# Fixing TensorE's written order through a block's heads, with split products in place of transposes

## The chip, the core and the metric

The kernel runs on one core of a Trainium2 chip. The metric is the time of one execution in microseconds (us) on the device, as a median of runs. PE is TensorE, PEld its weight loads, DVE is VectorE, ACT is ScalarE, POOL is GpSimd and SP is SyncE, which issues the DMAs of the weights.

## What is computed

Two transformer-like blocks on a sequence of 256 tokens with 2048 features, all in float32. The change lies in block 1's mixing stage, whose reference is, cut down:

```
h = rms_norm(x, ln1)
qkv_a, beta_a, decay_a, z_a, qkv_b, gate_a, gate_b = split(h @ w_in)
y_a = gated_deltanet(qkv_a, beta_a, decay_a, z_a, ...) @ w_branch_a
y_b = attention(rope(q_b), rope(k_b), v_b) @ w_branch_b
x = x + (sigmoid(gate_a) * y_a + sigmoid(gate_b) * y_b) @ w_out
```

`gated_deltanet` has 8 heads of 128 features. q, k and v come out of a causal convolution of width 4 and a SiLU; q and k are normed. Each head has per-token factors: beta (a sigmoid) and a decay g, whose running sum within a chunk is gc. Per chunk a triangular matrix built from k k^T, beta and exp(gc_i - gc_j) is inverted, and the state runs over the chunks. The head's output is normed and multiplied by silu(z). Attention has 8 heads too, causal, with one block of keys. A feed-forward part follows, and then the second block.

## The kernel before, in words

**Products.** Every large product is made from split operands: a weight chunk (512 KB, `load_w`, L322 to L326) is loaded on SP's queue into one of three buffers, ACT copies it rounded to `hi` (L325) and DVE subtracts to get `lo` (L326). The activations are held split as well. `wide_steps` makes 256 output columns feature-major: for each of 16 tiles of the contraction and each of two halves one product of 512 columns with `hi` and one of 256 with `lo` (L379, L381). `group_steps` makes 512 output columns token-major with three products of 512 columns each (L351 to L353). Both are generators. A yield tells how much PE work has been issued, 1.0 for a 512-column and a 256-column product together, and 2.0 for three of 512. Their results lie in one of two two-bank buffers (`pp`); small products use four single banks (`ps`).

**Fill.** The heads are long chains of small operations over PE, ACT and DVE. Between the steps of a chain the program issues large products of other tensors: `Fill` (L399 on) holds a list `todo` of such generators, `pull(n)` runs the first ones until `n` units of work are issued, `between(steps)` runs a chain and pulls as many units as each step yields, and `upto(gen)` finishes a generator.

**Order.** The program gives an order and a priority by it. The order on each engine is chosen by the compiler's scheduler, which simulates the engines and takes the first instruction in program order that is ready.

**Block 1's heads.** `gdn_proj(half)` makes q, k and v for four heads (two 256-column parts each for q, k and v) with a convolution per 128 features (`conv_silu`, L469 to L473: one ACT operation, three of DVE at L472, a SiLU). `z_proj(half)` makes silu(z) for four heads with 63 units. `gdn_gates` makes a 16-column product, transposes it (L524), computes beta and g on DVE and ACT (L526 to L552) and sums g by two products (L554, L555). `gdn_half(half)` then runs:

- `gdn_scales`: squares on ACT (L567), sums by products of one column (L571), and `rsqrt` on a 128x16 tile (L574 to L582), a chain of 13 short DVE operations to the factor `bk` (L579);
- four times `gdn_pre`: per head six transposes of a broadcast column (L592, L594), which spread gc, bk and rq over the rows of a PSUM tile; a masked exponential and three DVE operations that end in `aq` (L597 to L607);
- `inverse16`: the four heads' matrices go to DRAM and come back with one 16x16 block per partition; 15 steps of DVE (L707, L709) invert them; they return through DRAM into `Z`, and POOL spreads `Z` into `X` (L726);
- `gdn_inverse` in rounds over two head pairs: products and DVE steps that build the 64- and 128-row inverses (L735 to L770);
- `gdn_post` for two head pairs: seven steps (L628 to L670). After L651 comes the norm: squares on ACT, `rsqrt` on DVE, the scaling by silu(z) (L663), and then the transposes (L667).

The sequence (L903 on) is: `gdn_proj(0)`, gates, the other parameters, rope's angles; then z0, g1 (`gdn_proj(1)`) and z1 as fill for half 0; a0 and a1 (`attn_proj`) as fill for half 1 and heads 0 to 3 of attention; and `branch_a` (a gate product and a product that reads `oah` and `oal`, the heads' outputs) as fill for heads 4 to 7.

Of the kernel before, what the change touches and what calls it, by code (L numbers as in the profile page):

```python
# [122 lines left out]
def two_blocks_kernel(ctx: ExitStack, tc: tile.TileContext, I: dict, out: bass.AP):  # L123
# [29 lines left out]
    def c(name, lo=0, hi=128):  # L153
        return tabs[name][lo:hi]

    load_consts(0, cpool, nc.sync)
    ident, one = c("ident"), c("one")

# [17 lines left out]
    def tm(tag, F, dt=F32, bufs=2, p=128, pool=None):  # L176

        shape = list(F) if isinstance(F, (tuple, list)) else [F]
        n = math.prod(shape)
        line = {"tiny": LINE // 2, "rcol": LINE // 2, "PC": LINE // 4}.get(tag, LINE)  # L180
# [67 lines left out]
    def tiny(shape):  # L248
        return tm("tiny", shape, bufs=8)

# [148 lines left out]
    class Fill:  # L399
# [18 lines left out]

        def upto(self, gen):
# [11 lines left out]
    fills = Fill()  # L431

# [45 lines left out]
    def gdn_proj(half):  # L478
        kq[half] = [Q(3 * half + j, shape=(128, 2, 2, 2, 128), name="gdkq") for j in range(2)]
        vv[half] = Q(3 * half + 2, name="gdv")  # L480
        for j, part in enumerate("qkv"):
# [7 lines left out]
            def take(m, p):  # L489
# [6 lines left out]
            yield from wide_steps(w_in, f0 * 128, 512, xs, factors, take, place_x if r1 is None else None)  # L496
# [18 lines left out]
    def gdn_gates():  # L515
        ab = tm("cva", T, bufs=3)[:16]
        wide(w_in, 3072, 16, xs, None, lambda m, p: act(ab, p, AF.Copy))
        hp = wk("hp", (2, 8), bufs=1)
# [32 lines left out]
        for i in range(2):  # L551
            stt(g[:, i], t0[:, i], -1.0, ea, ALU.mult, ALU.mult)  # L552
        p = psum()
# [6 lines left out]
        stt(nbe, beta, -1.0, eg, ALU.mult, ALU.mult)  # L560

    def gdn_scales(half):
# [16 lines left out]
        tt(out=bk, in0=beta[:, :, hs], in1=rk, op=ALU.mult)  # L579
        tt(out=kdr, in0=kds[:, :, hs], in1=rk, op=ALU.mult)  # L580
        tt(out=nber, in0=nbe[:, :, hs], in1=rk, op=ALU.mult)
        tt(out=egq, in0=eg[:, :, hs], in1=rq, op=ALU.mult)  # L582
        return rk, rq, bk, kdr, nber, egq

    def gdn_pre(h, scales):
        half, m = divmod(h, 4)
        rk, rq, bk, kdr, nber, egq = scales
# [12 lines left out]
        tt(out=mg, in0=ga.unsqueeze(2).to_broadcast([128, 2, 2, 128]), in1=pb, op=ALU.mult)  # L600
# [19 lines left out]
    def gdn_post(h, scales, pre):  # L620
        half, m = divmod(h, 4)
        rk, rq, bk, kdr, nber, egq = scales
# [41 lines left out]
        yield  # L664
# [8 lines left out]
    def gdn_half(half):  # L673
        sc = gdn_scales(half)
        yield 12
# [165 lines left out]
    for _ in gdn_proj(0):  # L841
        pass
    load_consts(1, quad, nc.sync)
    gdn_gates()
# [63 lines left out]
    fills.add(a0, a1)  # L908
    fills.between(gdn_half(1))
    fills.upto(a0)  # L910
    fills.between(rounds(attn_head(h) for h in (0, 1)))
    fills.between(rounds(attn_head(h) for h in (2, 3)))
    fills.upto(a1)
    ba = [branch_a(j) for j in range(4)]
    fills.add(*ba)
    fills.between(rounds(attn_head(h) for h in (4, 5)))
    fills.between(rounds(attn_head(h) for h in (6, 7)))
    fills.upto(ba[3])
# [534 lines left out]
```

## Time and profile before

| | us |
|---|---|
| median of 3 runs | 2841.1 |
| lowest and highest of them | 2834.95, 2859.62 |
| the profiled execution | 2833.93 |
| its span, first to last instruction | 2832.2 |

The profile is of one execution. Its page gives the busy time of each engine and cuts the span into 40 equal slices. Groups of instructions are named by line and by the program's tile names, `out<-in`. A busy PE is modelled, since its products are pipelined: a 512-column product is shown with some 0.39 us, though the next starts 0.23 us after it. Start times, or the pieces on the chain of waits, show the rate. PEclk is the granted share of 2.4 GHz.

### The profile page before, as it was taken

What the parts mean: (1) busy time and instruction counts of PE and PEld (TensorE: products, weight loads), DVE (VectorE), ACT (ScalarE), POOL (GpSimd) and SP (SyncE); (2) the same over time, 40 slices, a digit from 0 to 9 for tenths busy, and PEclk for the clock granted to TensorE, in tenths of its full rate; (3) what the DMA queues carried; (4) which work ended last, traced back from release to release, by engine and by line L of the source; (5) the groups of instructions that cost most, each with busy time, mean ns of one, the idle gap of its engine ahead of it and who ended that gap; (6) DMA issues with size and microseconds to landing.
All of it is one profiled execution on the core that took longest, in us unless ns stands there. A gap on an engine that the chain in (4) does not pass through costs nothing.

```text
span 2832.2 us, 40520 instructions
## 1 busy us (share of the span) xinstructions
PE 2767.0 (98%) x15538; PEld 2329.3 (82%) x15538; DVE 1856.2 (66%) x2908; ACT 1397.8 (49%) x2088; POOL 159.2 (6%) x217
## 2 busy tenths in 40 slices
PE   9999989999999999999999999899999999999997
PEld 7888877888888888888887777777888888888886
DVE  7786766555577755775666696876765655656565
ACT  6664545444455544554455544334543444434454
POOL 0003200000000000000001120230000000000001
PEclk9999999999999999999999999899999999999999
DMA  7565644666566656655656363253566666666554
GB/s 218 165 177 150 173 137 119 185 187 186 186 186 189 191 189 188 187 187 190 203 188 183 101 159 108 77 142 105 176 192 193 187 191 191 188 193 204 186 186 149
DMA packets 398200, 487.94 MB, mean 172 GB/s; under 512 B 38426, under 2 KB 283173, under 8 KB 398005
## 3 DMA queue, kind: packets, MB, share of 16 engines
q1 hardware_dynamic: 397221, 482.93, 56.5%
q8 instruction: 122, 2.00, 0.3%
q10 hardware_dynamic: 608, 2.11, 0.2%
q0 software_dynamic: 176, 0.30, 0.1%
q14 instruction: 73, 0.60, 0.1%
HBM read 479.25 MB, written 6.03 MB: 171 GB/s over the span
## 4 chain that ended last, share of the span: by engine, by line
PE 91%; DVE 4%; DMA 2%; ACT 1%; issue 1%; POOL 1%; SPq 0%; DVEq 0%; POOLq 0%; ACTq 0%
PE pp L379 28%; PE pp L381 15%; PE pp L351 14%; PE pp L352 14%; PE pp L353 14%; DVE lo L326 1%; PE ps L267 1%; DMA Z<-s 0%; PE ps L742 0%; DMA raw<-in_w_down_dram 0%; PE ps L1215 0%; PE ps L735 0%; DVE L L1149 0%; PE ps L1217 0%; POOL X L726 0%
## 5 line engine op out<-in xcount | busy, mean ns | idle before, releaser
L326 DVE TENSOR_TENSOR lo<-raw,hi 128x1024 fp32r<-128x1024 f32 x902 | 1108.7, 1229 | 808.0 <-ACT hi L325 784.1
L325 ACT ACTIVATE hi<-raw 128x1024 fp32r<-128x1024 f32 x902 | 953.6, 1057 | 1195.1 <-PE pp L352 554.1
L379 PE MATMUL pp<-xhl,hi 128*128 128x512 f32 x3648 | 1291.7, 397 | 2.1 <-DVE z L388 2.1
L381 PE MATMUL pp<-xhl,lo 128*128 128x256 f32 x3648 | 1030.9, 283 | 2.3 <-DVE lo L326 2.3
L379 PEld LDWEIGHTS pp<-xhl,hi 128*128 128x128 f32 x3648 | 684.0, 188 | 164.7 <-DVE z L388 2.4
L381 PEld LDWEIGHTS pp<-xhl,lo 128*128 128x128 f32 x3648 | 688.8, 189 | 10.2 <-issue 4.7
L353 PE MATMUL pp<-lo,hid 128*128 128x512 f32 x864 | 338.2, 391 | 0.5 <-DVE lo L326 0.5
L351 PE MATMUL pp<-hi,hid 128*128 128x512 f32 x864 | 338.3, 392 | 0.0
L352 PE MATMUL pp<-hi,hid 128*128 128x512 f32 x864 | 337.6, 391 | 0.0
L353 PE MATMUL pp<-lo,xhl 128*128 128x512 f32 (+1 forms) x544 | 206.4, 379 | 0.0
L352 PE MATMUL pp<-hi,xhl 128*128 128x512 f32 (+1 forms) x544 | 206.3, 379 | 0.0
L351 PE MATMUL pp<-hi,xhl 128*128 128x512 f32 (+1 forms) x544 | 206.2, 379 | 0.0
L353 PEld LDWEIGHTS pp<-lo,hid 128*128 128x128 f32 x864 | 162.3, 188 | 35.9 <-DVE lo L326 1.0
L351 PEld LDWEIGHTS pp<-hi,hid 128*128 128x128 f32 x864 | 162.3, 188 | 35.1 <-ACT hi L325 0.3
L352 PEld LDWEIGHTS pp<-hi,hid 128*128 128x128 f32 x864 | 162.4, 188 | 34.3
L351 PEld LDWEIGHTS pp<-hi,xhl 128*128 128x128 f32 x544 | 102.6, 189 | 18.7
L352 PEld LDWEIGHTS pp<-hi,xhl 128*128 128x128 f32 x544 | 102.6, 189 | 18.4
L353 PEld LDWEIGHTS pp<-lo,xhl 128*128 128x128 f32 x544 | 102.5, 188 | 18.3
L933 DVE TENSOR_TENSOR x<-x,pp 128x512 f32<-128x512 f32 x96 | 61.6, 683 | 31.7 <-PE pp L353 31.7
L388 DVE TENSOR_TENSOR z<-pp,z 128x512 f32<-128x512 f32 (+2 forms) x119 | 80.8, 679 | 1.3 <-ACT z L387 1.1
L390 DVE TENSOR_TENSOR z<-z,rstd 128x512 f32<-128x512 f32 x114 | 78.4, 688 | 3.3
L287 POOL TENSOR_TENSOR junk<-x,rows 128x512 f32<-128x512 f32 x8 | 13.4, 1670 | 1110.2 <-ACT junk L284 1110.2
(415 smaller groups left out, 2535.7 us busy)
## 6 DMA issues: line engine op xcount, KB each, us to landing
raw<-in_w_in_dram SPq DMA_DIRECT2D x244, 512.0 KB, 3.6
raw<-in_w_up_dram SPq DMA_DIRECT2D x176, 512.0 KB, 4.4
raw<-in_w_ffn_up_dram SPq DMA_DIRECT2D x128, 512.0 KB, 3.7
raw<-in_w_ffn_down_dram SPq DMA_DIRECT2D x128, 512.0 KB, 4.1
raw<-in_w_down_dram SPq DMA_DIRECT2D x88, 512.0 KB, 3.7
raw<-in_w_out_dram SPq DMA_DIRECT2D x64, 512.0 KB, 3.7
raw<-in_w_ple_gate_dram SPq DMA_DIRECT2D x32, 512.0 KB, 3.9
raw<-in_w_branch_a_dram SPq DMA_DIRECT2D x16, 512.0 KB, 3.7
```

Of the source, the lines that this page charges most:

```text
L267: nc.tensor.transpose(p[:w, m - m0, i * 128:(i + 1) * 128], src[:, i, 128 * m:128 * m + w], ident)
L287: nc.gpsimd.tensor_tensor(out=y, in0=s, in1=self.w2[j], op=ALU.mult)
L325: act(h, r, AF.Copy)
L326: tt(out=l, in0=r, in1=h.bitcast(F32), op=ALU.subtract)
L351: mm(p, xh, h[:, j], start=(k == 0), stop=False, skip_group_check=True)
L352: mm(p, xl, h[:, j], start=False, stop=False, skip_group_check=True)
L353: mm(p, xh, l[:, j], start=False, stop=last, skip_group_check=True)
L379: mm(P[:w, m].rearrange("p a b -> p (a b)"), h[:, j, f], x2.rearrange("p a b -> p (a b)"), start=(k == 0), stop=False, skip_group_check=True)
L381: mm(P[:w, m, 0], l[:, j, f], x2[:, 0], start=False, stop=last, skip_group_check=True)
L388: tt(out=z, in0=P[:w, :nw, 0], in1=z, op=ALU.add)
L390: tt(out=z, in0=z, in1=r()[:w].unsqueeze(1).to_broadcast([w, nw, T]), op=ALU.mult)
L933: tt(out=s, in0=s, in1=p, op=ALU.add)
```

## The change

- `pe_in_order()` opens a stretch, from the gates to the last `branch_a`, in which PE's instructions keep the order in which the program issues them. The other engines' order is still the scheduler's.
- The numbers that steps yield are new, and some steps yield that did not: the gates 6, 40 and 0; the scales 4 for each of four squares, 14 and 4; after `inverse16` 88 in place of 55; and 6 per head more at the norm of `gdn_post`.
- `gdn_gates` moves behind the other parameters and rope's angles, and runs with fill between its steps.
- The fill of half 0 is g1's six parts, now six generators, then z0 and z1. When `inverse16` has been issued, `fills.first(z0, z1)` puts z0 and z1 right behind the part that is under way.
- The token factors are no longer spread by transposes of broadcast columns. POOL gathers gc, bk and rq of four heads in a table `S`; two transposes turn it, ACT and DVE split it into `RT` (hi and lo), and per head and factor two products of 256 columns, with a broadcast column of a rounded identity (`picks`) as the weights, spread a row of it. The six transposes per head go.
- Two small tiles (`nacc`, `oka`) are padded less, and the squares of `gdn_scales` have two buffers (tag A) in place of one (tag E).

```diff
+    picks = cpool.tile([128, LINE], F32R, tag="picks", name="picks")
+    nc.scalar.activation(picks, ident[:, :LINE], AF.Copy)
...
+    def spread_table(S):
+        p = psum()
+        for i in range(2):
+            nc.tensor.transpose(p[:, i * 128:(i + 1) * 128], S[:, i], ident)
+        RT = wk("RT", (2, T), F32R, bufs=1)
+        split(RT[:, 0], RT[:, 1], p[:, :T])
+        return RT
+
+    def spread_row(p, RT, sel):
+        mm(p, sel, RT[:, 0], start=True, stop=False, skip_group_check=True)
+        mm(p, sel, RT[:, 1], start=False, stop=True, skip_group_check=True)
...
+        def first(self, *gens):
+            self.todo = self.todo[:1] + list(gens) + [g for g in self.todo[1:] if g not in gens]
...
+    def pe_in_order():
+        return tc.manual_schedule(engines={mybir.EngineType.PE})
...
-            yield from wide_steps(w_in, f0 * 128, 512, xs, factors, take, place_x if r1 is None else None)
+            for o in range(2):
+                yield wide_steps(w_in, f0 * 128 + 256 * o, 256, xs, factors, lambda m, p, o=o, take=take: take(2 * o + m, p),
+                                 (lambda k, o0, o=o: place_x(k, o)) if r1 is None else None)
...
     def gdn_gates():
         ab = tm("cva", T, bufs=3)[:16]
         wide(w_in, 3072, 16, xs, None, lambda m, p: act(ab, p, AF.Copy))
+        yield 6
...
+        yield 40
         p = psum()
         mm(p[:, 0:16], c("upper"), g, start=True, stop=True)
...
     def gdn_scales(half):
...
-            sq = wk("E", (2, 2, 128), bufs=1)
+            sq = wk("A", (2, 2, 128))
             act(sq, kq[half][m // 2][:, m % 2], AF.Square)
+            yield 4
...
+        S = wk("E", (2, 128), bufs=1)
+        nc.gpsimd.memset(S, 0.0)
+        nc.gpsimd.tensor_copy(S[:, :, 0:4], gc[:, :, hs])
+        nc.gpsimd.tensor_copy(S[:, :, 4:8], bk)
+        nc.gpsimd.tensor_copy(S[:, :, 8:12], rq)
...
-        return rk, rq, bk, kdr, nber, egq
+        yield 14
+        RT = spread_table(S)
+        yield 4
+        return (rk, rq, bk, kdr, nber, egq), RT
...
     def gdn_pre(h, scales):
...
-        pa, pb = psum((2, 128)), psum((2, 2, 128))
-        for i in range(2):
-            nc.tensor.transpose(pa[:, i], gc[:, i, h:h + 1].to_broadcast([128, 128]), ident)
-            for j, f in enumerate((bk, rq)):
-                nc.tensor.transpose(pb[:, i, j], f[:, i, m:m + 1].to_broadcast([128, 128]), ident)
+        pa, pb = psum(T), psum((2, T))
+        for j, p in enumerate((pa, pb[:, 0], pb[:, 1])):
+            spread_row(p, RT, picks[:, 4 * j + m:4 * j + m + 1].to_broadcast([128, 128]))
...
     def gdn_post(h, scales, pre):
...
             stt(ot[:, i], ot[:, i], ro[:, i:i + 1], zs[half][:, i, 128 * m:128 * m + 128], ALU.mult, ALU.mult)
-        yield
+        yield 6
...
-    def gdn_half(half):
-        sc = gdn_scales(half)
-        yield 12
+    def gdn_half(half, *light):
+        sc = yield from gdn_scales(half)
         pre = []
         for m in range(4):
             pre.append(gdn_pre(4 * half + m, sc))
             yield 5
         Z = inverse16([p[0][:, 0] for p in pre], 2)
-        yield 55
+        fills.first(*light)
+        yield 88
         for _ in rounds(gdn_inverse(pre[m:m + 2], Z[:, m:m + 2]) for m in (0, 2)):
             yield 6
         for m in (0, 2):
-            for _ in rounds(gdn_post(4 * half + m + i, sc, pre[m + i]) for i in range(2)):
-                yield 5
+            for n in rounds(gdn_post(4 * half + m + i, sc, pre[m + i]) for i in range(2)):
+                yield 5 + n
...
-    z0, z1, g1, a0, a1 = z_proj(0), z_proj(1), gdn_proj(1), attn_proj(0), attn_proj(1)
-    fills.add(z0, g1, z1)
-    fills.pull(30)
-    fills.between(gdn_half(0))
-    fills.upto(z1)
+    z0, z1, g1, a0, a1 = z_proj(0), z_proj(1), list(gdn_proj(1)), attn_proj(0), attn_proj(1)
+    with pe_in_order():
+        fills.add(*g1, z0, z1)
+        fills.between(gdn_gates())
+        fills.between(gdn_half(0, z0, z1))
+        fills.upto(z1)
+        fills.upto(g1[-1])
...
```

From there on the calls are those of before, inside the stretch, up to `fills.upto(ba[3])`.

## Rows read from the trace of the kernel before

**Rows 1.** The page: busy us, share of the span and instructions of each engine.
```profile
PE 2767.0 (98%) x15538; PEld 2329.3 (82%) x15538; DVE 1856.2 (66%) x2908; ACT 1397.8 (49%) x2088; POOL 159.2 (6%) x217
```

**Rows 2.** Windows: us from:to, length, busy us of each engine (instructions), clock, DMA share, GB/s.
```profile
60.00:80.00 20.00, 20.00 (x117) 17.66 (x116) 14.92 (x23) 11.44 (x18) 0.00 (x0) 1.00 0.67 170
400.00:442.00 42.00, 30.22 (x305) 24.65 (x304) 25.23 (x102) 18.29 (x54) 2.21 (x2) 0.80 0.18 53
560.00:580.00 20.00, 20.00 (x89) 16.48 (x88) 9.30 (x8) 8.58 (x9) 0.00 (x0) 1.00 0.66 202
```

**Rows 3.** Waits of PE from 395 to 445 us: total us, times, longest us.
```profile
PE ps L667 <- DVE e L663: 7.9, 2, 4.0
```

**Rows 4.** PE in order of time: start us, us, what, idle time before and its cause.
```profile
168.20 1.03 PE L604 MATMUL ps<-gdkq 128*128 128x256 f32 x4
...
415.12 0.78 PE L651 MATMUL ps<-d,aq 128*128 128x128 f32 x4
419.82 0.74 PE L667 MATMUL ps<-C,e 128*128 128x128 f32 x2 [3.92 <-DVE e L663]
421.18 0.80 PE L351 MATMUL pp<-hi,oah 128*128 128x512 f32 x1 [0.62 <-ACT oah L669]
...
424.33 0.42 PE L352 MATMUL pp<-hi,oal 128*128 128x512 f32 x1
...
433.93 0.74 PE L667 MATMUL ps<-C,e 128*128 128x128 f32 x2 [3.98 <-DVE e L663]
...
441.37 0.43 PE L352 MATMUL pp<-hi,xhl 128*128 128x512 f32 x1
```

**Rows 5.** Chain of waits in a pre step: start us, us on the chain, what.
```profile
361.56 0.44 PE ps L594 x4
...
368.23 0.86 PE ps L604 x4
```

**Rows 6.** All engines in order of time, around the gates.
```profile
87.35 0.27 PE L381 MATMUL pp<-xhl,lo 128*16 128x256 f32 x1
...
91.13 0.40 ACT L517 ACTIVATE cva<-z 16x256 f32<-16x256 f32 x1
...
96.29 0.23 DVE L526 TENSOR_SCALAR abt<-ps,rcol 128x16 f32<-128x16 f32 x1 [0.31 <-PE ps L524]
...
113.51 0.24 DVE L552 SCALAR_TENSOR_TENSOR G<-G,ea 128x8 f32<-128x8 f32 x2
```

**Rows 7.** Groups of DVE by line: busy us, mean ns of one, idle before.
```profile
L326 DVE TENSOR_TENSOR lo<-raw,hi 128x1024 fp32r<-128x1024 f32 x902 | 1108.7, 1229 | 808.0 <-ACT hi L325 784.1 <-PE ps L267 13.8 <-PE pp L352 4.2
L388 DVE TENSOR_TENSOR z<-pp,z 128x512 f32<-128x512 f32 (+2 forms) x119 | 80.8, 679 | 1.3 <-ACT z L387 1.1
...
L472 DVE SCALAR_TENSOR_TENSOR cva<-z,PT,cva 128x255 f32<-128x255 f32 (+2 forms) x72 | 30.5, 476 | 0.6 <-ACT cva L469 0.6
```

**Rows 8.** DVE in order of time, scales of both halves, a pre step.
```profile
137.39 0.17 DVE L574 TENSOR_SCALAR tiny<-ps 128x16 f32<-128x16 f32 x1 [1.41 <-PE ps L571]
...
148.06 0.16 DVE L579 TENSOR_TENSOR gsc<-G,gsc 128x8 f32<-128x8 f32 x1
...
338.37 0.69 DVE L240 TENSOR_SCALAR tiny<-tiny 128x16 int32<-128x16 int32 x1
...
345.46 0.16 DVE L579 TENSOR_TENSOR gsc<-G,gsc 128x8 f32<-128x8 f32 x1
...
363.78 0.87 DVE L607 SCALAR_TENSOR_TENSOR aq<-ps,gsc,A 128x256 f32<-128x256 f32 x2
```

**Rows 9.** POOL in order of time, around both inverses.
```profile
202.91 0.63 POOL L711 COPY Ei<-Ei 64x256 f32<-64x256 f32 x1 [112.63 <-DVE Ei L709]
211.03 3.52 POOL L726 TENSOR_TENSOR X<-Z,C 128x512 f32<-128x512 f32 x2 [7.49 <-DMA Z<-s]
...
391.41 1.51 POOL L711 COPY Ei<-Ei 64x256 f32<-64x256 f32 x1 [35.93 <-DVE Ei L709]
398.71 3.50 POOL L726 TENSOR_TENSOR X<-Z,C 128x512 f32<-128x512 f32 x2 [5.79 <-DMA Z<-s]
```

More of the change, by code (lines that the diff above doesn't have):

```diff
@@ L179, in tm @@
         n = math.prod(shape)
-        line = {"tiny": LINE // 2, "rcol": LINE // 2, "PC": LINE // 4}.get(tag, LINE)
+        line = {"tiny": LINE // 2, "rcol": LINE // 2, "PC": LINE // 4, "nacc": LINE // 2, "oka": LINE // 2}.get(tag, LINE)
         t = (pool or tmp).tile([p, -(-n // line) * line], dt, tag=tag, name=nm(tag), bufs=bufs)[:, :n]
@@ L487, in factors, with take @@
                 return r1s
-            def take(m, p):
+            def take(m, p, part=part, f0=f0, j=j):
                 if part == "v":
@@ L560, in gdn_gates @@
         stt(nbe, beta, -1.0, eg, ALU.mult, ALU.mult)
+        yield 0
     def gdn_scales(half):
@@ L582, in gdn_scales @@
         tt(out=egq, in0=eg[:, :, hs], in1=rq, op=ALU.mult)
-        return rk, rq, bk, kdr, nber, egq
+        yield 14
+        RT = spread_table(S)
+        yield 4
+        return (rk, rq, bk, kdr, nber, egq), RT
     def gdn_pre(h, scales):
         half, m = divmod(h, 4)
-        rk, rq, bk, kdr, nber, egq = scales
+        (rk, rq, bk, kdr, nber, egq), RT = scales
         KQ, v = kq[half][m // 2][:, m % 2], vv[half][:, m]
-        pa, pb = psum((2, 128)), psum((2, 2, 128))
-        for i in range(2):
-            nc.tensor.transpose(pa[:, i], gc[:, i, h:h + 1].to_broadcast([128, 128]), ident)
-            for j, f in enumerate((bk, rq)):
-                nc.tensor.transpose(pb[:, i, j], f[:, i, m:m + 1].to_broadcast([128, 128]), ident)
+        pa, pb = psum(T), psum((2, T))
+        for j, p in enumerate((pa, pb[:, 0], pb[:, 1])):
+            spread_row(p, RT, picks[:, 4 * j + m:4 * j + m + 1].to_broadcast([128, 128]))
+        pa = pa.rearrange("p (i c) -> p i c", i=2)
         ga = wk("ivp", (2, 128))
@@ L599, in gdn_pre @@
         mg = wk("A", (2, 2, 128))
-        tt(out=mg, in0=ga.unsqueeze(2).to_broadcast([128, 2, 2, 128]), in1=pb, op=ALU.mult)
+        tt(out=mg, in0=ga.unsqueeze(2).to_broadcast([128, 2, 2, 128]), in1=pb.rearrange("p j (i c) -> p i j c", i=2),
+           op=ALU.mult)
         pg = psum((2, 2, 128))
@@ L621, in gdn_post @@
         half, m = divmod(h, 4)
-        rk, rq, bk, kdr, nber, egq = scales
+        rk, rq, bk, kdr, nber, egq = scales[0]
         KQ = kq[half][m // 2][:, m % 2]
@@ L839, in attn_head @@
         yield 3
-    for _ in gdn_proj(0):
-        pass
+    for part in gdn_proj(0):
+        for _ in part:
+            pass
     load_consts(1, quad, nc.sync)
-    gdn_gates()
     other_params()
@@ L901, in branch_b @@
         feature_major(mg[j], 512, lambda m, p: split(mh[j][:, m], ml[j][:, m], p))
-    z0, z1, g1, a0, a1 = z_proj(0), z_proj(1), gdn_proj(1), attn_proj(0), attn_proj(1)
-    fills.add(z0, g1, z1)
-    fills.pull(30)
-    fills.between(gdn_half(0))
-    fills.upto(z1)
[L908 to L918, printed above, removed]
+    z0, z1, g1, a0, a1 = z_proj(0), z_proj(1), list(gdn_proj(1)), attn_proj(0), attn_proj(1)
[5 more added lines that the diff above has]
+        fills.upto(g1[-1])
+        fills.add(a0, a1)
+        fills.between(gdn_half(1))
+        fills.upto(a0)
+        fills.between(rounds(attn_head(h) for h in (0, 1)))
+        fills.between(rounds(attn_head(h) for h in (2, 3)))
+        fills.upto(a1)
+        ba = [branch_a(j) for j in range(4)]
+        fills.add(*ba)
+        fills.between(rounds(attn_head(h) for h in (4, 5)))
+        fills.between(rounds(attn_head(h) for h in (6, 7)))
+        fills.upto(ba[3])
     obb = pairs([obh[i] for i in range(2)], [obl[i] for i in range(2)])
```

## The prediction, made before the changed kernel ran

> **What bounds the kernel now.** I read the page first: TensorE (PE) is busy for 98% of the span, the next engine for 66% [rows 1]. So time can only come from stretches in which PE waits or runs slowly. The page's 40 slices show hardly any, so I went on to windows, and one stretch of the heads stands out [rows 2]: from 400 to 442 us PE is busy for 30.22 of 42.00 us, idle for 11.8, at a mean granted clock of 0.80. All slices from 20 to 400 us show 20.00 busy of 20.00 as that from 60 to 80 does. The waits name a cause [rows 3]: two of 4.0 us, where the transposes of a finished head pair (L667) wait for VectorE's last scaling (L663). PE's order in time shows why that hurts [rows 4]: after L651 at 415.12 there is nothing left to put in. The next big product (L351, branch a) itself reads what the heads deliver, and starts at 421.18. The same happens a pair later. Behind each idle stretch the clock is at 1.2 instead of 2.4 GHz (products 0.43 us apart instead of 0.23): from 419.82 to 424.33 and from 433.93 to 441.37, 12.0 us, of which half, 6.0, is lost. So the stretch loses 11.8 + 6.0 = 17.8 us, 0.6% of the time.
>
> **The unit.** A number that a step yields is paid in products: one of 512 and one of 256 columns for 1.0. At 117 products in 20 us a pair takes 0.342 us; at 89 in 20 us one of 512 columns takes 0.225 [rows 2], so one of 256 takes 0.117.
>
> **What the written order removes.** Before, the scheduler chose PE's order, and by 400 us it had spent a0, a1 and two gates while half 1 still had its inverses and posts ahead. Now the order is fixed. Half 1 asks for 34 (scales) + 20 (pre) + 88 + 8 x 6 (inverse) + 2 x 52 (posts) = 294 units, and a0 and a1 hold 2 x (4 x 32 + 63) = 382. Of the 88 left, heads 0 to 3 take 84; heads 4 to 7 have branch a's 376. Half 1 cannot run dry, so the 17.8 us go: 12 if only the idle time goes, 20 if some of what passes for busy in that stretch goes too. What is late next there is the norm chain, 4.7 us from L651 to L667 [rows 4], behind 5 + 17 units = 7.5 us.
>
> Half 0 does run dry. It asks for 46 (gates) + 294 = 340, but six parts of g1 at 32 and two z at 63 are 318. The 22 that lack are the last two 5s and 12 of the last norm step's 17. z0 itself is ready 91 units after inverse16, ahead of the posts.
>
> **What it adds, term by term** (low / taken / high, in us). In a written order all products behind a waiting instruction wait too, and with them the weight buffers, ScalarE's (ACT) and VectorE's (DVE) conversions and SP's loads. So each term is a chain's length less its cover in units.
>
> *Spread on PE.* Per head six transposes of 128 columns, 0.11 us each (four in 0.44), become six products of 256 columns at 0.117: 48 x 0.007 = 0.3, and four transposes for tables 0.4. Taken 0.7; at the 0.215 of a plain fp32 product of that width (L604, four in 0.86) [rows 5] it is 48 x 0.105 + 0.4 = 5.4. I take the rate of the split product of 256 columns, the same type and width. 0 / 0.7 / 5.4.
> The Trainium skill speaks against this edit: "Perfetto Trace Analysis", section Transposes, asks for transposes rather than ordinary products, since these skip the arithmetic. Taken so, the edit would stand at its 5.4 and the whole at 2840.1; no row shows a split product on a broadcast column, so the rows make it unlikely but do not refute it.
>
> *picks, padding, S.* One 32-column activation, nearest a copy at 0.40 [rows 6], at a time when PE waits for its first data; the paddings issue nothing; POOL's memset of S lies beside 16 units of squares. 0 / 0.2 / 0.7.
>
> *Gates, first transpose (L524).* The last 16-column product ended at 87.62 and its copy at 91.53: 3.9 us, behind weight conversions on both engines [rows 6]. Cover 6 units = 2.05. other_params' small loads now stand ahead in SP's queue. 0 / 0.8 / 1.9.
>
> *Gates, cumulative sums (L554).* From 96.29 to 113.75, 17.5 us [rows 6], beside rope's angles and under z's products, which bring only weight subtractions. Rope, some 5 us of it, is now issued ahead; but g1's first convolution falls in, two operations on z at 0.68 and six L472 at 0.476 [rows 7], 4.2 us. Cover 40 units = 13.7. From 12.5 to 17.5: 0 / 0.8 / 3.8.
>
> *Scales of half 0.* The rsqrt chain ran from 137.39 to the factor bk at 148.22, 10.8 us under g1's convolutions [rows 8]. Its cover is 14 units = 4.8, and g1's second part ends there (unit 64; the cover is 62 to 76). New are POOL's copies of bk and rq behind it: one took 0.63, and 1.51 in half 1 [rows 9]; these are far smaller, so 0.3 to 1.5 in all. Free, the chain is 13 operations 0.2 apart, 2.6, and with two weight subtractions of 1.23 [rows 7] 5.1. Once PE stands no new weights come, so I take a value well below the middle. 0.6 / 2.0 / 7.5.
>
> *Scales of half 1.* About the same chain took from 338.37 to 345.62, 7.3 us, its first operation 0.69 beside rope on POOL and not 0.17 [rows 8]. 0 / 1.2 / 4.0.
>
> *Table split, twice.* Between table and first spread stand a copy and a subtraction of 256 columns, 0.40 each by the nearest row [rows 6]; behind a weight conversion on each engine 3.1. Cover 4 units = 1.4. 0 / 1.0 / 3.4.
>
> *Eight pre steps.* From L594 at 361.56 [rows 5] to aq's end at 364.65 [rows 8] the chain is 3.1 us. The step's own products, nine at 0.11 and four at 0.215, and 5 units are 1.85 + 1.7 = 3.55. A step uses all four PSUM buffers, so a late aq holds up the next. 0 / 1.2 / 8 (a weight subtraction in the way each time is 0.8).
>
> *Inverse.* In half 1 from L604 at 368.23 [rows 5] to half of POOL's X at 400.5 [rows 9] it took 32.2 us; cover 5 + 88 + 6 units = 33.9. In half 0, with g1's convolutions on DVE, from 168.20 [rows 4] to 212.8 [rows 9], 44.6. Now 28 units of g1 remain there, then z: one convolution, 32.2 + 4.2 = 36.4. 0 / 0.5 / 10.7, nearer to half 1's rows since z loads DVE as those do.
>
> *End of half 0.* The 4.7 us from L651 to L667 [rows 4] were on a DVE with no weights. Cover 5 + 5 units = 3.4, and g1's last convolution (4.2) and a subtraction end there too. 1.3 / 2.5 / 6.7, and 2.2 more if the clock falls as it did behind 3.9 idle us.
>
> *All other rounds.* Inverse rounds have 2.05 us of cover, posts 1.7, other norm steps 7.5, heads 8.9; against them a copy of 0.40 and one weight subtraction. 0 / 1.2 / 6.
>
> Sum taken: 0.7 + 0.2 + 0.8 + 0.8 + 2.0 + 1.2 + 1.0 + 1.2 + 0.5 + 2.5 + 1.2 = 12.1. Net -17.8 + 12.1 = -5.7 us. The profiled execution took 2833.9 (span 2832.2), so it would be 2828.2; the median of the runs shown is 7.2 higher, and a median of runs comes to 2841.1 - 5.7 = 2835.4. Work saved on DVE (66%) or ACT (49%) [rows 1] counts for nothing here. Outside the heads nothing is edited: 0.
>
> **Rivals.**
> *A, every wait is covered.* Then the low ends 0.6 and 1.3 and the 0.7 on PE stay: -17.8 + 2.6 = -15.2, 2825.9. For it: a standing PE takes the weights off DVE. Against it: the scales' chain exceeds its cover even without a convolution (5.1 against 4.8).
> *B, slower: half 0's short chains stand in line behind g1's convolutions.* g1 now runs beside gates, scales and the last post, where z or nothing did, and DVE puts 4.2 us at a time between operations of chains with 13.7, 4.8, 1.4 and 3.4 us of cover. Price: 3.8 + 7.5 + 1.7 + 6.7 + 2.2 = 21.9 for the 0.8 + 2.0 + 0.5 + 2.5 = 5.8 taken: +16.1, net +10.4, 2851.5. It decides once these waits pass 5.8 + 5.7 = 11.5 us. For it: the chains of 17.5 and 10.8 us. Against it: these were stretched under products that never stopped.
> *C, the order does not hold what it counts on.* The other engines' order still comes from the scheduler; if that puts chains ahead of weight conversions, PE lacks weights in place of work. At the size of the gain this returns it: 2841.1, no change. Against it: with a fixed order the scheduler knows when weights are due.
>
> **How the numbers follow.** Forecast 0.50, A 0.22, B 0.22, C 0.06. The runs shown lie 0.9% apart, so about 1%, 28 us, can be told from no change. Faster by that is more than the 17.8 and needs a gain elsewhere: 0.04. Slower by it needs B and the high ends of pre and inverse together: 0.08. Same 0.88. Range: from A less 8 us of spread among runs, 2818, to B plus 8.5, 2860; about 2 in 10 lie outside.
>
> **What would show it.** Right: clock 1.00 and products between L651 and L667 in half 1's posts, 7.5 us apart; a wait of 2 to 3 us at the end of half 0 and at the first table; six spread products per head 0.12 us apart. Wrong: over 4 us idle at gates or scales with the clock below 0.9; idle time before half 0's first L735; a dip that has only moved to the heads; or another time for the feed-forward part, which I count as unchanged.

## The result: slower by 1.6%, and the profile after

| | before | after |
|---|---|---|
| median of 4 runs each, us | 2849.2 | 2885.38 |
| lowest and highest, us | 2834.95, 2859.62 | 2882.88, 2890.1 |
| ratio, 95% interval | | 1.0156, 1.0122 to 1.019 |
| span of the profiled execution, us | 2832.2 | 2882.1 |
| its 9,500th large product from the last starts at, us | 782.3 | 826.8 |

The quotient of the two medians is 1.0127, within the interval of the ratio: two of the four runs of before lie 16 us and more above the other two, as some of its later runs do, but none of e7, e14 and e15 below.

The last line is a mark behind block 1's heads: it is the same product in every kernel here. The profiled execution is 49.9 us longer; 44.5 us of that are there when the heads end, and some 6 us come in the last feed-forward layer. The forecast was 5.7 us faster, and its range ended at 2860.

The page of the changed kernel, busy us of each engine, answers to [rows 1]:

```profile
PE 2786.5 (97%) x15542; PEld 2338.8 (81%) x15542; DVE 1859.2 (65%) x2910; ACT 1387.0 (48%) x2082; POOL 163.2 (6%) x225
```

Shares of the whole span hardly move, and nothing can be read from them. The windows can, against [rows 2]. Windows of PE in the changed kernel: from:to, length, busy us (instructions), clock, DMA share, GB/s:

```profile
60.00:80.00 20.00, 20.00 (x115) 1.00 0.65 168
80.00:100.00 20.00, 17.13 (x90) 0.91 0.44 129
...
120.00:140.00 20.00, 16.60 (x94) 0.91 0.40 117
...
180.00:200.00 20.00, 15.52 (x194) 0.83 0.38 97
...
220.00:240.00 20.00, 17.21 (x97) 0.91 0.45 131
240.00:260.00 20.00, 12.53 (x76) 0.89 0.47 132
...
320.00:340.00 20.00, 11.91 (x70) 0.77 0.56 152
...
380.00:400.00 20.00, 14.55 (x73) 0.83 0.36 99
400.00:420.00 20.00, 15.79 (x82) 0.83 0.39 112
420.00:440.00 20.00, 20.00 (x115) 1.00 0.55 157
```

Before, one dip of 42 us stood alone. It is gone from its place (from 420 us on the windows are full), and in place of it eight windows have less than 18 us busy. The clock falls in each of them. The waits say what PE stood for. Waits of PE in the changed kernel from 60 to 520 us: total us, times, longest us, against [rows 3]:

```profile
PE ps L706 <- DVE e L702: 19.6, 8, 4.3
PE ps L775 <- POOL X L766: 13.0, 2, 8.0
PE ps L257 <- POOL E L614: 4.3, 2, 3.4
PE ps L551 <- ACT cva L543: 2.9, 1, 2.9
PE pp L397 <- DVE lo L342: 0.6, 2, 0.3
...
```

With a last one of 0.3 they come to 40.7 us, where [rows 2] had 11.8 us of idle time. (L706 is L667 of before, L775 is L735, L766 is L726; L257 are the table's transposes, L551 those of the gates.) But for the 0.6 us, in which weights were late, large products stand next in PE's order, and it may not take them. At the end of half 0 (7.1 us of the norms' 19.6) the list of fill had run out, as the prediction said it would: 10 of the 22 units stood ahead of the transposes, and the next products were issued behind them.

The waits and the clock behind them account for the mark. Between 60 and 560 us PE was idle for 40.7 us, and busy for 36.1 us at a granted clock of 0.50, which costs 18.0: 58.7 us in all. In the kernel before it was 11.4 + 5.4 = 16.9. The difference is 41.8 us. Of the 44.5 at the mark 1.8 were there at 59 us, ahead of the heads, which leaves 42.7 to explain.

One norm shows it, against [rows 4]. PE in order of time at the last norm of half 1's first pair: start us, us, what, idle time before:

```profile
402.31 0.60 PE L690 MATMUL ps<-d,aq 128*128 128x128 f32 x4
402.67 0.47 PE L395 MATMUL pp<-xhl,hi 128*128 128x512 f32 x1
...
410.27 0.28 PE L397 MATMUL pp<-xhl,lo 128*128 128x256 f32 x1
414.19 0.74 PE L706 MATMUL ps<-C,e 128*128 128x128 f32 x2 [3.64 <-DVE e L702]
415.50 0.74 PE L706 MATMUL ps<-C,e 128*128 128x128 f32 x2 [0.58 <-DVE e L702]
415.89 0.77 PE L395 MATMUL pp<-xhl,hi 128*128 128x512 f32 x1
416.46 0.41 PE L397 MATMUL pp<-xhl,lo 128*128 128x256 f32 x1
```

The 22 units ran from 402.67 to 410.55, 7.9 us, as forecast (7.5). The chain was not 4.7 us: the first head's transposes stood at 414.19, and the second head's 1.3 us later. Behind the wait a pair of products takes 0.79 us (415.89 to 416.68, where the next pair starts) and not 0.342: the lower clock, granted at 0.50 from 412.6 to 419.4 us. VectorE at the same time, start us, us, what:

```profile
406.77 0.67 DVE L242 TENSOR_SCALAR tiny<-tiny 128x2 int32<-128x2 int32 x1
407.47 0.66 DVE L243 TENSOR_SCALAR tiny<-tiny 128x2 int32<-128x2 int32 x1
408.17 0.65 DVE L245 TENSOR_TENSOR tiny<-tiny 128x2 f32<-128x2 f32 x1
...
408.74 1.21 DVE L342 TENSOR_TENSOR lo<-raw,hi 128x1024 fp32r<-128x1024 f32 x1
...
411.17 0.16 DVE L242 TENSOR_SCALAR tiny<-tiny 128x2 int32<-128x2 int32 x1
...
412.17 1.23 DVE L342 TENSOR_TENSOR lo<-raw,hi 128x1024 fp32r<-128x1024 f32 x1
...
413.78 0.61 DVE L702 SCALAR_TENSOR_TENSOR e<-e,tiny,zs 128x128 f32<-128x128 f32 x2
```

Two weight subtractions lie between the chain's steps, and the second head's steps too. The same operation on two columns took 0.67 us at 406.77 and 0.16 at 411.17; GpSimd was rotating at the first, and idle from 411.22 on (start us, us, what):

```profile
405.99 0.72 POOL L818 TENSOR_TENSOR qb<-qb,rope 32x256 f32<-32x256 f32 x1 [18.95 <-DVE cva L817]
406.68 0.73 POOL L819 TENSOR_TENSOR cva<-cva,rope 32x256 f32<-32x256 f32 x1
407.38 0.72 POOL L818 TENSOR_TENSOR qb<-qb,rope 32x256 f32<-32x256 f32 x1
...
408.76 2.46 POOL L820 TENSOR_TENSOR qb<-qb,cva 32x256 f32<-32x256 f32 x2
```

Half 1's inverse, against [rows 9]: the products on X (L775) began 45.0 us after the last Gram product (the last of four at L643, 290.06, to 335.01 us), where the same stretch of before took 31.7 (368.71 to 400.42). PE and then GpSimd there, start us, us, what:

```profile
289.42 1.02 PE L643 MATMUL ps<-gdkq 128*128 128x256 f32 x4
...
335.01 2.34 PE L775 MATMUL ps<-X,aq 64*64 64x64 f32 x32 [7.99 <-POOL X L766]
```

```profile
321.36 1.71 POOL L818 TENSOR_TENSOR qb<-qb,rope 32x256 f32<-32x256 f32 x1
...
326.60 1.60 POOL L751 COPY Ei<-Ei 64x256 f32<-64x256 f32 x1
...
333.69 2.48 POOL L766 TENSOR_TENSOR X<-Z,C 128x512 f32<-128x512 f32 x2 [2.88 <-DMA Z<-s]
```

VectorE finished the last of the 15 steps at 321.19, and the copy began at 326.60, behind rotations.

### The profile page after: what moved, and what is told of

It reads as the page before. It is cut to its first block, busy times and chain, and to the rows that moved or that the text cites. A ratio compares the mean times of both kernels' runs of the same rounds, so it can differ in the third digit from the quotient of the medians.

```text
span 2882.1 us, 40544 instructions
## 1 busy us (share of the span) xinstructions
PE 2786.5 (97%) x15542; PEld 2338.8 (81%) x15542; DVE 1859.2 (65%) x2910; ACT 1387.0 (48%) x2082; POOL 163.2 (6%) x225
## 4 chain that ended last, share of the span: by engine, by line
PE 88%; DVE 7%; DMA 2%; ACT 1%; POOL 1%; issue 1%; SPq 0%; ACTq 0%; DVEq 0%; POOLq 0%
PE pp L395 27%; PE pp L367 14%; PE pp L368 14%; PE pp L369 14%; PE pp L397 14%; DVE lo L342 2%; PE ps L283 1%; DMA Z<-s 1%; PE ps L782 1%; ACT hi L341 0%; DVE L L1191 0%; DVE ivp L747 0%; DVE cva L496 0%; POOL X L766 0%; PE ps L775 0%
## 5 line engine op out<-in xcount | busy, mean ns | idle before, releaser
L369 PEld LDWEIGHTS pp<-lo,hid 128*128 128x128 f32 x864 | 162.6, 188 | 36.6
L368 PEld LDWEIGHTS pp<-hi,hid 128*128 128x128 f32 x864 | 162.6, 188 | 36.4
L367 PEld LDWEIGHTS pp<-hi,xhl 128*128 128x128 f32 x544 | 103.2, 190 | 19.2
```

The lines of the kernel that those rows point to most:

```text
L367: mm(p, xh, h[:, j], start=(k == 0), stop=False, skip_group_check=True)
L368: mm(p, xl, h[:, j], start=False, stop=False, skip_group_check=True)
L369: mm(p, xh, l[:, j], start=False, stop=last, skip_group_check=True)
```

## The experiments

The mark is the start of the 9,500th large product from the last in the profile; it is free of what block 2 does, where nothing was edited and where the times scatter (the runs of before alone lie between 2831.87 and 2859.62 us). The mark itself has some us of scatter: at 59 us, ahead of the heads, the profiles lie 0.3 to 2.9 us behind before's.

In the traces two things differ behind the mark, both between 1540 and 2030 us, in block 2. First, an edit in block 1 can change the order that the scheduler gives block 2: e7, e14 and e15 have one and the same order there on PE, DVE, ACT and POOL, in which 1,259 of PE's 11,261 instructions behind 800 us stand in another place than in before; e5 and e10 have before's order there. Second, the clock can fall there. Windows of PE, first before, then e10:

```profile
1580.00:1600.00 20.00, 20.00 (x97) 1.00 0.29 80
```

```profile
1580.00:1600.00 20.00, 20.00 (x46) 0.50 0.19 53
```

e10 loses 14 us against before in that place (1548 to 1609 us of before), in the same order. So a total or a ratio holds more than the edit did to the heads.

| kernel | mark, us | span, us | ratio to before |
|---|---|---|---|
| before | 782.3 | 2832.2 | 1 |
| after | 826.8 | 2882.1 | 1.0156 [1.0122, 1.019] |
| e1 after, scheduler's order | 791.3 | 2845.7 | 1.0042 [1.0027, 1.0057] |
| e2 before, written order | 848.0 | 2897.7 | 1.0241 [1.0207, 1.0275] |
| e3 after, 16 at the norms | 814.2 | 2878.5 | 1.0146 [1.0131, 1.0161] |
| e4 after, v parts behind half 1's inverse | 822.4 | 2878.9 | 1.0156 [1.0141, 1.0171] |
| e5 before, with after's places in memory | 785.3 | 2842.9 | 1.0011 [0.9984, 1.0038] |
| e6 after, transposes kept | 824.5 | 2879.9 | one run |
| e7 before, one gate in another slot | 782.3 | 2826.4 | 0.9954 [0.9931, 0.9978] |
| e8 after, numbers from measured chains | 796.7 | 2855.5 | 1.0059 [1.0038, 1.008] |
| e10 before, two lines halved | 785.5 | 2854.6 | 1.0011 [0.9982, 1.004] |
| e11 before, two gates ahead | 784.6 | 2854.5 | 1.0001 [0.9971, 1.0032] |
| e12 as e8, spread and places of before | 779.4 | 2834.5 | 1.0013 [0.9986, 1.0041] |
| e13 after, rotation on VectorE | 831.3 | 2890.2 | one run |
| e14 new numbers alone | 788.4 | 2834.6 | 0.998 [0.9963, 0.9997] |
| e15 is e7 again | 781.6 | 2832.0 | 0.9959 [0.9938, 0.998] |

**e1: the order taken away.**

```diff
-        return tc.manual_schedule(engines={mybir.EngineType.PE})
+        return ExitStack()
```

> The changed kernel with everything in it but the written order of TensorE: the scheduler orders block 1's heads again. Theory 1 (TensorE stands in line behind chains that are longer than their numbers: its waits for the norms, the X of the inverse, the factor table and the gates add to 40.1 us between 60 and 520 us of the changed kernel, and the clock falls behind the long ones): nearly all of the loss goes, the time is 0.995 to 1.003 of the kernel before, and the wait of the norms' transposes falls from 19.6 to under 8 us. Rival 2 (the new work itself costs: the split products of the spread, the table, the z projections out of their old place): the time stays at 1.012 or above. Rival 3 (the chains are slow because VectorE and GpSimd are crowded by the moved fill, whatever the order): something between, 1.005 to 1.012, with the chain from the last Gram product to X still over 40 us in half 1.

35.5 of the 44.5 us at the mark go (826.8 to 791.3), and the norms' wait is 7.9 us. The total is 1.0042, between theories 1 and 3; the chain from the last Gram product to X took 36.6 us in half 1, not over 40, which speaks against theory 3. 9.0 us at the mark stay, 2.9 of them from ahead of the heads.

**e2: the order alone.**

```diff
-    fills.add(z0, g1, z1)
+    with tc.manual_schedule(engines={mybir.EngineType.PE}):
+        fills.add(z0, g1, z1)
...
```

> The kernel before with nothing but the written order of TensorE round block 1's heads: its old numbers between steps, its transposes for the spread, z ahead. Theory 1: the old numbers give the inverse 55 units (18.8 us at 0.342 us) and the norms 10 units (3.4 us) where the chains of the changed kernel took 40 to 45 us and 8 to 12 us, so TensorE waits 20 to 25 us at each inverse and about 5 us at each of the four pairs of norms, and the clock falls behind each: 60 to 110 us more than before, 1.02 to 1.04. The order alone is then worse than the change, whose new numbers give part back. Rival 2 (the order costs nothing, the new work does): 0.995 to 1.005 of the kernel before.

As theory 1 had it: 65.7 us at the mark, 1.0241; but the inverses waited 10 us each, not 20 to 25, since their chains took 33.7 and 34.9 us here. The longest waits of PE in this kernel from 60 to 560 us:

```profile
PE ps L735 <- POOL X L726: 20.6, 2, 10.9
PE ps L667 <- DVE e L663: 19.2, 8, 5.3
PE ps L554 <- DVE G L552: 9.1, 1, 9.1
PE ps L571 <- ACT E L567: 5.6, 6, 1.8
...
```

The inverse waits 20.6 us behind 55 units; the change's 88 units bring it to 13.0. The gates' 9.1 are gone behind 40, the squares' 5.6 with a second buffer and 4 units a square. The norms stay at 19.2 against 19.6, although their cover rose from 10 to 22 units. The order costs, and the rest of the change gives 21 us of it back at the mark.

**e3: more in front of the norms.**

```diff
-        yield 6
+        yield 16
         pt = psum()
```

> The changed kernel with 16 in place of 6 ahead of the norms' transposes, so that 37 units (12.7 us) stand there for a pair of heads in place of 17 (5.8 us); nothing else. Theory 1: the wait of the norms' transposes falls from 19.6 us to 5 to 10 us (in half 0 the products that are left run out sooner, so the last pair there still waits), and the time falls by 8 to 14 us, 1.011 to 1.013 of the kernel before. Rival 3 (the products that are put in between bring weights to prepare on VectorE and so lengthen the chain by what they cover): the wait stays above 15 us and the time within 3 us of the changed kernel.

The norms' wait fell from 19.6 to 7.6 us, as theory 1 had it, and the mark by 12.6, although 3.4 us of waits appear at attention's transposes (L870), whose fill the norms have spent. The ratio is above the 1.011 to 1.013 that was expected: in the profile the stretch from mark to end took 9.0 us longer than in the changed kernel, though nothing in it was edited. So the norms' price is confirmed at the mark and not by the ratio. The longest waits of PE in this kernel from 60 to 560 us:

```profile
PE ps L775 <- POOL X L766: 12.5, 2, 6.9
PE ps L706 <- DVE e L702: 7.6, 4, 6.2
PE ps L257 <- POOL E L614: 4.3, 2, 3.4
PE ps L870 <- DVE A L866: 3.4, 2, 2.3
...
```

**e4: half 1's inverse beside quiet fill.**

```diff
-        fills.add(a0, a1)
-        fills.between(gdn_half(1))
+        a0, a1 = list(attn_proj(0)), list(attn_proj(1))
+        fills.add(*a0, *a1)
+        fills.between(gdn_half(1, a0[2], a1[2]))
...
```

> The changed kernel with the attention projections cut into q, k and v parts, and the two v parts put behind half 1's inverse as z0 and z1 are behind half 0's; the rotating q and k parts come later. Theory 3 for the inverse (half 1's chain took 44.6 us because a0's q and k parts lie beside it: their evacuation on VectorE, and their rotation on GpSimd ahead of the copy and X in its queue): last Gram product to first product on X falls to 32 to 36 us, that wait from 8.0 to under 2 us, the clock between 320 and 340 us from 0.77 to above 0.95, and the time by 6 to 14 us. Rival: the chain is long by its DMAs and its 15 steps whatever lies beside: it stays over 40 us and the time within 3 us. A way to lose: the rotating parts now lie beside half 1's norms and slow those, and the wait of the norms' transposes grows by what the inverse gains.

A miss by size: from the last Gram product to the first product on X 39.8 us in place of 45.0, not 32 to 36; the waits for X fell from 13.0 to 8.1 us (half 1's from 8.0 to 2.7, not under 2), the mark by 4.4. `first` lets the part that is under way end first, so some of a0's rotating work stays beside the inverse.

**e13: the rotation off GpSimd.**

```diff
-        nc.gpsimd.tensor_tensor(out=d, in0=d, in1=rope[:, 0], op=ALU.mult)
+        tt(out=d, in0=d, in1=rope[:, 0], op=ALU.mult)
...
```

> The changed kernel with the three products of each rotation on VectorE in place of GpSimd. Theory P (GpSimd's queue: in the changed kernel the copy of half 1's inverse was ready at 321.2 us and ran at 326.60 behind rotation steps of 1.7 to 2.4 us, and VectorE's small steps took 0.5 to 0.7 us beside them): from the last Gram product to the first product on X 36 to 40 us in place of 45.0, its wait from 8.0 to under 4 us, and the span 3 to 8 us under 2882.1. Rival (VectorE's load, which this adds to): 44 us or more and the span the same or longer.

The rival: 47.2 us, and a span 8.1 us longer. VectorE now began half 1's 15 steps at 303.68 and ended them at 334.13 us, 30.4 us, where they took 21.4 (299.75 to 321.19); the copy followed at once. So the 5.4 us in GpSimd's queue were there, but here the work beside the chain lengthened it on VectorE by more (9.0 us). Both are from one run each.

**e5 and e10: places in memory.** e5 has both of these edits on the kernel before, e10 the second alone.

```diff
+    picks = cpool.tile([128, LINE], F32R, tag="picks", name="picks")
+    nc.scalar.activation(picks, ident[:, :LINE], AF.Copy)
...
-"PC": LINE // 4}.get
+"PC": LINE // 4, "nacc": LINE // 2, "oka": LINE // 2}.get
```

> The kernel before with nothing of the change but its places in memory: the picks tile is made (and not used), and the lines of the nacc and oka tiles are halved. The changed kernel is 43.9 us behind before at the end of block 1's heads and 50 us at its end; in its last stretch the spacing of the 512-column products has a median of 231 ns against 227 ns before, and the kernel with the old body in the written order has 227 ns as well. Theory L (the places of the operands in memory set that spacing): 231 ns here too in the last feed-forward layer, and 3 to 8 us over before, 1.001 to 1.003. Rival (the tail is slower by what the heads leave behind, such as which buffers are in use or the order of the queues): 227 ns and 0.999 to 1.001.

> The kernel before with the lines of nacc and oka halved and no picks tile: what lies in the small-tile pool behind them moves by 64 bytes, what lies in the pools ahead of it (x, the split activations, the weights) stays where it was. In the kernel before with both, the 512-column products of the last stretch had a median spacing of 231 ns against 227 ns. If the 128 bytes that the picks tile adds ahead of activations and weights make that spacing, it is 227 ns here and the span within 3 us of before's 2832.2 us. Rival (it is the 64 bytes in the small-tile pool): 231 ns and 6 to 11 us over.

The ratios (1.0011 both) tell nothing, the rows do. Groups of PE by line from 2100 to 2780 us: first e10, then e12, which has the places of before; busy us, mean ns of one:

```profile
L353 PE MATMUL pp<-lo,hid 128*128 128x512 f32 x512 | 202.3, 395 | 0.0
L351 PE MATMUL pp<-hi,hid 128*128 128x512 f32 x512 | 202.3, 395 | 0.0
```

```profile
L365 PE MATMUL pp<-hi,hid 128*128 128x512 f32 x512 | 199.5, 390 | 0.0
L367 PE MATMUL pp<-lo,hid 128*128 128x512 f32 x512 | 199.5, 390 | 0.0
```

By their starts the 1,536 products of this kind lie 227.1 ns apart on average in the kernel before and in e12, and 232.7 in e5, e10 and the changed kernel: 1,536 x 5.6 ns = 8.6 us, of which some 3 come back in the layer's wide products (236 to 232 ns). Theory L holds, and the 64 bytes in the small-tile pool suffice; the picks tile is not needed for it. That is the changed kernel's loss in its tail, some 6 us. At the mark e5 and e10 are 3.0 and 3.2 us behind before, but 1.0 and 1.5 of that they were at 59 us, ahead of the heads.

**e6 and e14: the spread.** e6 puts the six transposes back into the changed kernel; e14 does so too, and takes out the order and the places in memory.

```diff
-        RT = spread_table(S)
         yield 4
...
+        for i in range(2):
+            nc.tensor.transpose(pa[:, i], gc[:, i, h:h + 1].to_broadcast([128, 128]), ident)
```

> The changed kernel with the token factors spread by six transposes a head as before, no table, its numbers and written order kept. If the spread by split products costs by its table in the written order (the table's transposes wait 4.3 us in two places, the clock is 0.91 between 120 and 140 us behind the longer one): that wait is gone or under 1 us, 120 to 140 us runs at 0.98 or above, and the span is 4 to 9 us under the changed kernel's 2882.1 us. Rival (the same chain of square sums and rsqrt holds the spread, whichever way it is done): the first transpose of a head waits in its place, and the span is within 3 us.

> The changed kernel without its written order, its split products, its table and its places in memory: the new numbers, the gates in among the fill and z behind the inverse, under the scheduler's order. At the end of the heads the changed body under the scheduler was 6 us behind the kernel with its places in memory alone. If the spread by split products and its table cost that: level with before, 0.997 to 1.002, heads within 2 us. If the new numbers and z's place cost it: 4 to 9 us behind at the end of the heads, 1.001 to 1.004.

e6: the rival. The table's 4.3 us are gone, and 2.4 us for `mg` (L633) and 1.3 for the factors stand in their place; the span is 2.2 us shorter. e14: the second answer at the mark, 6.1 us behind before; the total came out at 0.998. e1 is 6.0 behind e5, and differs from it by numbers, z and split products; e14 is 6.1 behind before by numbers and z alone. So split products and table are worth nothing that shows under the scheduler. The numbers cost some 4 us at the mark there: of the 6, e14 had 2.5 at 59 us, ahead of the heads, and e1 1.9 more than e5.

**e7, e11, e15: the stall of before by another way.**

```diff
-        dst = sg[j] = halves(Q(7, name="sg"))
+        dst = sg[j] = halves(Q(slot, name="sg"))
...
-        yield from gate(7184, j)
+        yield from gate(7184, j, 7 if j else 15)
```

> The kernel before with one slot changed: the first gate of branch a goes into slot 15, which is free, in place of slot 7, where z1 lies until half 1's last norm. Theory D (the stall of before between 400 and 442 us, 11.8 us idle and 6.0 us at half clock by the prediction, is a lack of products that are free to run: the gate's 64 units stand blocked by their slot): gate products lie between half 1's last steps, and the first pair of norms' wait of 4.0 us goes with part of the slow clock: 6 to 14 us less, 0.995 to 0.998. Rival (the chains end the heads whatever is ready, and what is filled in here is missing behind): within 3 us of before.

> The kernel before with the first gate of branch a in slot 15, and the second gate set ahead of the first product of the branch (slot 7, so that it may gather its sums but not leave PSUM before half 1's last norm). With the first gate alone 0.9954 was measured, and 4.4 us of waits at the norms stayed, with the clock at 0.81 between 440 and 460 us. Theory D (a lack of products that are free to run): 64 more units lie ready for the last pair of heads, the remaining wait falls under 2 us, the clock there is above 0.95, and the time is 0.991 to 0.995. Rival (only what can leave PSUM helps, or the scheduler puts the second gate elsewhere): 0.995 to 0.997 as with one gate.

> The kernel before with branch a's first gate in slot 15, once more. In the first run the profile ended the heads at the same time as before (its 9,500th product from the last began at 782.3 us in both) and the 5.8 us came in block 2, where nothing was changed. If the gain is one of the runs and not of the edit: 0.998 to 1.002 now, and the heads end level again. If the edit brings it in some way: 0.993 to 0.997 again.

Windows of PE in e7, as above:

```profile
400.00:420.00 20.00, 17.93 (x216) 0.91 0.51 155
420.00:440.00 20.00, 17.91 (x108) 1.00 0.29 87
440.00:460.00 20.00, 14.36 (x72) 0.81 0.32 99
```

A gate's products fill the first norm's wait, the stall moves from 420 to 440 us, and the mark is where it was (782.3). At the heads the rival is right: products filled in here are missing at the next norm. It is not the first gate that fills, as theory D had it: its 96 products had run by 395 us in the kernel before too. There its sums could leave PSUM only at 436.5 us (the sigmoid, L880), and in e7 they do at 397.7; the second gate's products then run from 404 to 446 us. With two gates ahead (e11) the second gate's products are spent by 427 us, both norms wait 4.0 us again, and from 440 to 460 us PE is busy for 10.77 us at a clock of 0.75; the mark is 784.6.

Yet e7 was measured twice at 0.9954 and 0.9959. Its profile gains 5.7 us on before's, all of it between 1438 and 2024 us, where its order in block 2 is the other one; e15's profile gains 0.1 (2833.8 us, the slowest of its eleven runs, whose median is 2828.64). So this is a version that beats both kernels by 0.4%, and not by its heads. The other order of block 2 is what differs where the profile gains; that it brings the gain was not tried by itself.

**e8 and e12: the written order with numbers from chains that were measured.**

```diff
-        yield 88
+        yield 100
...
-        fills.add(*g1, z0, z1)
+        a0, ga0 = list(attn_proj(0)), gate(7184, 0)
+        fills.add(*g1, z0, z1, *a0[:2])
...
```

> The changed kernel in its written order, with numbers and fill sized by the chains that the profile of the changed kernel shows: 14 for 6 ahead of the norms' transposes, 100 for 88 ahead of the inverse's products, 24 for 14 ahead of the table, 16 for 6 ahead of the gates' transposes; the v parts behind half 1's inverse; q and k of a0 brought into half 0 and a gate of branch a into half 1 (slots 15 and 7 change places), so that the fill lasts. Theory 1 (it is the numbers, not the order as such): TensorE's waits between 60 and 560 us fall from 40.7 to under 15 us, the clock stays above 0.95 in nearly every 20 us, and the time is 0.995 to 1.005 of before. Rival (in the written order every chain grows with the fill that is laid beside it, and TensorE waits all the same): over 25 us of waits and above 1.010.

> The written order with numbers and fill by the measured chains (as in the run with 14, 100, 24 and 16), with 110 and 52 in place of 100 and 40 where waits of 4.4 and 4.2 us were left, and with the spread by transposes and the places in memory of before: no picks, no table. Theory 1 with theory L: the places in memory were worth 7 to 11 us of that run's 1.0059 and the two larger numbers some 5 to 8 us, so the time is 0.995 to 1.002 of before: the written order can stand level with the scheduler's, not ahead of it by more than the stall at 400 to 442 us. Rival (the written order loses by itself): 1.004 or above.

The diff is e8's, cut down; e12 has 110 and 52 besides. e8's waits came to some 20 us, where under 15 were expected, and the mark to 796.7; 1.0059, 0.1% above what was expected. e12 has its mark at 779.4, 2.9 us ahead of before, at 1.0013, which is level. PE is idle for 11.9 us in it between 60 and 560 us, as in the kernel before (11.4), and loses 1.7 us to the clock where before loses 5.4. Half of X was ready 44 and 37 us after the last Gram product: the chains are longer than the 31.7 us of before's half 1, but covered. Two waits and two windows of e12 (L698 is the norms' transposes, L767 the product on X):

```profile
PE ps L698 <- DVE e L694: 4.9, 3, 2.3
PE ps L767 <- POOL X L758: 2.1, 2, 1.5
```

```profile
400.00:420.00 20.00, 19.19 (x100) 1.00 0.58 175
420.00:440.00 20.00, 20.00 (x95) 1.00 0.51 151
```

So the written order does not lose by itself. It loses where a number is smaller than its chain, and with the chains covered it gained nothing here that shows in the total.

## Why the prediction was wrong

**What the order removes: right as to products, wrong in what followed.** "Half 1 cannot run dry, so the 17.8 us go": the dip at 400 to 442 us did go, and large products stood ready at every wait. But PE could stand in line as well as run dry, and does so in eight windows. The new numbers alone do not remove the dip: under the scheduler (e14) both waits of 4.0 us at the norms stay. Nor did more products shorten the heads: e7 only moved the dip. And by 400 us before had spent one gate, not two; its sums held one of the two `pp` buffers until 436.5 us.

**The terms that failed** are *Inverse*, *All other rounds* and *End of half 0*.

- *Inverse* was taken at 0.5 us with a high end of 10.7. It is 5.0 + 8.0 = 13.0. The step that failed is "it took 32.2 us; cover 5 + 88 + 6 units = 33.9": that length had been read where the scheduler laid other work beside it. With a0's evacuations, conversions and rotations beside it the same chain took 45.0, and the other runs show that it moves with what lies beside it (34.9 in e2, 36.6 in e1, 39.8 in e4, 47.2 in e13). In half 0 the 36.4 reckoned was 40.3.
- *All other rounds* was taken at 1.2, high end 6. The norms' waits are 19.6 in all; 7.1 of them (4.10 and 3.03, a transposed head each) belong to *End of half 0* (taken 2.5, high end 6.7 before the clock), and 12.5 to this term, with 0.9 of small waits besides. The 4.7 us from L651 to L667 were one chain on a VectorE without weights. In a written order the cover is made of products whose weights VectorE prepares, two heads run their chains at once, and GpSimd rotates: 11.9 us in the rows above, against 7.5 of cover. e3 shows that these were the norms and what they cost: 12.6 us at the mark for 20 units a pair.

**The clock was priced once, at 2.2 us.** Of the dip of before a third was clock (6.0 of 17.8), and this share belonged on each term with a long wait. Summed over the windows from 80 to 420 us, 20 us times what the clock lacks to 1.00 is 24 us; 18.0 of it fell in busy time.

**Smaller terms.** *Spread on PE* was right: where the clock is up, the products follow each other by 0.113 to 0.118 us (0.117 taken), and by 0.213 at the first head (131.12 to 132.19 us), behind the table's wait, where it is down. By the rule of the Trainium skill, "Perfetto Trace Analysis", section Transposes, to make transposes as transposes, the prediction had priced the edit at 5.4 us; putting the transposes back (e6) shortened the span by 2.2 in one run, and under the scheduler nothing shows, so the trace does not bear the 5.4 out here. *Scales* 3.4 and 0.9 for 2.0 and 1.2, near. *Gates, first transpose* 2.9 for 0.8, above its high end. *Cumulative sums*, *eight pre steps* and *table split* showed no wait of over 0.1 us: their chains were covered. "Outside the heads nothing is edited: 0" missed the two halved lines, worth some 6 us in the tail.

**The rivals.** B was on the right side and named the mechanism, short chains in line behind other work on VectorE, with a threshold of 11.5 us. In the four places that it named the waits came to 3.4 + 7.1 = 10.5 us, so by its own account it would just not have decided. It looked in half 0 and for g1's convolutions alone, and the larger part came from the inverses and half 1's norms; its 2851.5 was a quarter of the way to what came. C did not show itself: PE waited 0.6 us for weights.

What stays open: which of the new numbers costs the some 4 us at the mark under the scheduler, why the lines of two small tiles change the spacing of products, and whether block 2's other order by itself makes e7 and e14 better in total than at the mark.

## What to carry to other kernels

Before fixing an engine's order, list each chain's length as it will be with the new fill beside it, not as it was read under the scheduler: the fill's own conversions, evacuations and rotations run on the engines that the chain needs, and here they made 32 us into 45 and 5 into 12. Price every uncovered wait with its clock behind it. And first run the order alone (e2) and the rest alone (e1): two runs told which half of the edit cost 35 us.

## What the runs showed of the hardware that was not expected

- Halving the lines of two small tiles changed the spacing of 512-column products in the last feed-forward layer from 227.1 to 232.7 ns on average. Which operand's place does it was not tried.
- VectorE's two-column operations took 0.67 us while GpSimd rotated, and 0.16 us right after. In the rows above both engines start a step every 0.69 to 0.70 us: they take turns. GpSimd's steps took 0.72 us there and 1.71 at 321.36, while VectorE ran weight subtractions (1.35 us at 321.12). The Trainium skill, "SBUF — State Buffer", section "SBUF: two separate sides", says that these two engines share a pair of ports that one operation holds for its whole length, on VectorE's side if it runs in a two-port mode or has two inputs in SBUF. The turns in the rows agree with such a lock; whether L242 and L243, which have one input, ran in such a mode no row shows. The prediction had the 0.69 in its own [rows 8] and did not carry it to the norms.
